# A heads' loop in a written order for TensorE, with dt's columns in the values' product

## The chip, the cores and the metric

The kernel runs on one core of one Trainium2 chip. The metric is the device time of one execution in microseconds, the median of three runs.

## What is computed

The reference is a chain of transformer blocks on 512 tokens of width 1024 in fp32: first a block with a pooling mixer, sparse attention, attention to a memory and a gated feed-forward, and then two hybrid layers. Only the hybrid layers are touched here. Each of them computes, from the same input `h`:

```python
proj = einsum("bld,de->ble", x, w_in)
q, k, v, z_attn, z_ssm, xbc, dt_raw = split(proj, ...)   # 1024, 256, 256, 1024, 1024, 1536, 16 columns
attn = sliding_window_attention(q, k, v, sinks) * silu(z_attn)
xbc = silu(causal_depthwise_conv(xbc, conv_w, conv_b))   # width 4
xs, bm, cm = split(xbc, ...)                             # 1024, 256, 256 columns
dt = softplus(dt_raw + dt_bias); a = -exp(a_log)         # 16 heads
# in chunks of 128 tokens, 2 groups of 8 heads, head width 64, state 128:
a_cs = cumsum(dt * a)                                    # within a chunk
y_diag = (cb * exp_segsum(a_cs)) @ (xs * dt)             # cb = C B^T
states = B^T @ (exp(a_cs_last - a_cs) * xs * dt)         # carried from chunk to chunk: prev
y_off  = (C @ prev) * exp(a_cs)
ssm = gated_rmsnorm(y_diag + y_off + xs * d_skip, z_ssm, ssm_norm_w)
out = concat([attn, ssm]) @ w_out                        # then a layer norm of ALPHA * x + out
```

## The kernel before, in words

Activations lie with channels on the 128 partitions and the 512 tokens along the free dimension, as eight tiles. Every fp32 operand of a projection is split into a high and a low part, and a projection of 128 output channels, called a unit here, is 24 products of 128x128 by 128x512: eight times high by high and high by low (L149, L150 in `mm3`) and eight times low by high (L154). A unit's weights come by one transfer of 512 KB on SyncE's queue (L104 in `weights`), are cast to the high part by ScalarE (L107) and give the low part by two VectorE subtractions of 512 columns (L110). There are three buffers each for the raw weights, the high and the low parts. PSUM has eight banks: four named mm for units, two named lg and two named tr.

A planner orders the instructions of TensorE, VectorE, ScalarE and GpSimd at build time by its own estimate of durations, with program order as the priority. Only SyncE's queue keeps program order (`manual_schedule` in `build`). Each engine then runs its list in order.

`hybrid(L)` goes through these steps.

1. The weights of dt (16 columns) are loaded and split into `wdt` (L914 to L919).
2. Four gate units (z_ssm) are done in two halves of 256 tokens with their weights held (`units_by_k`); `silu` follows (tanh on ScalarE, L211, and one VectorE operation, L911).
3. dt: 16 products of 128x48 by 128x512 (L931) into a tile of 16 partitions by 512 tokens, with the channels' high and low parts side by side. Softplus, the product with a, and the cumulative sum (a VectorE scan, L949) run on 16x512 tiles. The cumulative sum and its exponential are written to DRAM (`acsd`, L951, L953). Eight small transposes (L959, L960) bring dt and the sum to tokens on partitions (`dtok`, `atok`); `cdec` and `dend` follow.
4. Convolutions: `conv(j)` is a unit, one ScalarE operation that reads it (L900), three VectorE operations (L902), tanh (L211), and a last VectorE operation (L905). B and C take four, xs eight. cb (L979) and the transposes of B (L990) stand between them.
5. `tokens(g)` for each group of eight heads: for four chunks, four transposes of xs (L1007) into a tr bank, from which VectorE makes `xdt` (L1010) and, for three chunks, `xe` (L1014); a state product (L1016) into an lg bank, and VectorE's two operations that carry the state on (L1021, L1022).
6. `decay_rows(j)` asks on SyncE's queue for the broadcast rows of two heads (L1030, L1031). `decay(j)` makes exp of the clipped difference: four operations of 128 columns per head, on ScalarE (L1057) or, for the first head of a pair from the fourth pair on, on VectorE (L1055), an exponential (L1058), and a product with cb on GpSimd for the first and VectorE for the second head of a pair (L1059).
7. `heads(j)` for a pair of heads: eight products (L1070, recorded as 16) and three (L1076, recorded as 6), each group into a tr bank, and three VectorE operations (L1078, L1079, L1080). The product with the gate (L1110) and the sum of squares (L196, L199, with GpSimd's addition L200) follow; `gated_norm` runs once for each four pairs.
8. The loop over eight pairs holds seven more units: three convolutions and four gates. After it come two units for the keys (split to four tiles each, with copies between partition halves asked for on ScalarE's queue, L1126), then the values: tokens on the output partitions, 96 products of 128x128 by 128x256 (L1139 to L1141), then the second gated norm and the first queries' unit.
9. The attention loop (`scores`, `transposed`, `values`), and the output projection.

Of the kernel before, what the change touches and what calls it, by code (L numbers as in the profile page):

```python
# [61 lines left out]
class Kern:  # L62
# [79 lines left out]
    def mm3(self, out, w, xs, m=P, start=True, stop=True, woff=0):  # L142
# [732 lines left out]
    def l2_consts(self):  # L875
# [4 lines left out]
        self.small = self.load("small16", [16, 4], nc.sync)  # L880

    def hybrid(self, L):
# [4 lines left out]
        e16 = lambda: self.f("G")[:16, :]  # L887
        xr, e, uu, sm, dtf, acs, seg = (e16() for _ in range(7))
        nc.scalar.dma_start(seg, a["segs"])

# [4 lines left out]
        def conv(j, tag, w=None):  # L895

            y, o = self.f("ht"), self.f(tag)
            cw = lambda w: cwh[:, w * 12 + j : w * 12 + j + 1]
            pt = self.proj(W[4 + j], h, w=w)
# [17 lines left out]
        nc.gpsimd.memset(wdt.bitcast(F32), 0.0)  # L917
        w3, wd3 = wdt.rearrange("p (k m) -> p k m", m=48), wd.rearrange("p (k m) -> p k m", m=16)
        self.split(wd3, w3[:, :, :16], w3[:, :, 32:])  # L919

# [11 lines left out]
        nc.scalar.activation(xr, pt[32:48], AF.Identity, bias=self.small[:, L : L + 1])  # L932
        nc.vector.tensor_tensor(xr, pt[:16], xr, ALU.add)
        BC = [conv(8 + j, "R") for j in range(4)]
# [9 lines left out]
        nc.vector.scalar_tensor_tensor(dtf, xr, 0.0, uu, ALU.max, ALU.add)  # L944
        av = self.s("av", (16, 1), 2)
        nc.scalar.activation(av, self.small[:, 2 + L : 3 + L], AF.Exp)
        nc.vector.tensor_scalar(av, av, -1.0, None, ALU.mult)
        nc.vector.tensor_scalar(e, dtf, av, None, ALU.mult)
        nc.vector.tensor_tensor_scan(acs, seg, e, 0.0, ALU.mult, ALU.add)  # L949
# [48 lines left out]
        xdt = {}  # L998
        prevs = {}

        def tokens(g):

            for c in range(4):
                cc = slice(c * P, (c + 1) * P)
# [424 lines left out]
```

## Time and profile before

| | us |
|---|---|
| median of three runs (lowest, highest) | 1649.32 (1648.4, 1650.72) |
| the profiled execution | 1650.6 |
| its span, first to last instruction | 1648.8 |
| its mean granted clock of TensorE | 0.994 |

The span is what the trace shows; 1.8 us lie around it. In the stretch from about 800 us on the granted clock is 1.00 in the windows shown. A row of TensorE's timeline gives an instruction's start and duration; products overlap, so what a product costs is the distance of two starts. A number in brackets behind a row is the idle time of that engine just before it, and what ended it.

### The profile page before, as it was taken

Reading aid. Unit: us, or ns where it says so; the run is one execution under the profiler, and the core shown is the slowest. Engines: PE = TensorE matmul, PEld = TensorE weight load, DVE = VectorE, ACT = ScalarE, POOL = GpSimd, SP = SyncE. Lnnn points to the kernel's source line nnn. Section 1 sums busy time; section 2 is a strip of 40 time slices with the busy share of each in tenths; the row PEclk is TensorE's granted clock in tenths of the full one; section 3 lists DMA queues with packets and bytes.
Section 4 is the critical chain, followed back from the end, with each engine's and each line's share of the span. In section 5 each row is a group of like instructions: output and inputs, shape, how many; then the busy total and the mean of one; then the engine's idle time right before and its main releaser. Section 6 shows DMA issues by size and latency. Waiting matters only on the chain. (4 is left out here: it accounts for less than half of the span.)

```text
span 1648.8 us, 24498 instructions
## 1 busy us (share of the span) xinstructions
PE 1601.2 (97%) x9014; PEld 1358.7 (82%) x9014; DVE 1140.7 (69%) x2490; ACT 805.5 (49%) x1571; POOL 212.4 (13%) x251
## 2 busy tenths in 40 slices
PE   8999999999999999999999999999999989999996
PEld 5778888889898888888998778887998867888786
DVE  6779967547886455533767998765497799777447
ACT  4543245336863333323556556665355555666424
POOL 2000213000100000000000121211230022111131
PEclk9999999999999999999999999999999999999998
DMA  6522332243233323234636223211452522322133
GB/s 222 198 97 76 120 103 64 77 158 116 81 116 111 102 92 100 89 104 119 196 124 191 80 77 103 78 65 51 141 171 81 178 87 78 102 78 65 64 103 116
DMA packets 66233, 180.28 MB, mean 109 GB/s; under 512 B 7953, under 2 KB 19169, under 8 KB 66113
## 3 DMA queue, kind: packets, MB, share of 16 engines
q1 hardware_dynamic: 56320, 166.75, 31.8%
q10 hardware_dynamic: 9792, 11.96, 2.4%
q8 instruction: 71, 1.16, 0.3%
q14 instruction: 50, 0.40, 0.1%
HBM read 170.14 MB, written 9.06 MB: 109 GB/s over the span
## 5 line engine op out<-in xcount | busy, mean ns | idle before, releaser
L149 PE MATMUL psmm<-G,whi 128*128 128x512 f32 (+2 forms) x1244 | 479.2, 388 | 2.2 <-ACT whi L107 2.2
L110 DVE TENSOR_TENSOR wlo<-wraw,whi 128x512 fp32r<-128x512 f32 x515 | 358.8, 718 | 174.8 <-ACT whi L107 123.8
L150 PE MATMUL psmm<-G,whi 128*128 128x512 f32 (+2 forms) x1244 | 473.6, 384 | 0.0
L107 ACT CAST whi<-wraw 128x1024 fp32r<-128x1024 f32 (+3 forms) x262 | 267.7, 1024 | 339.7 <-PE psmm L150 272.3
L154 PE MATMUL psmm<-G,wlo 128*128 128x512 f32 (+2 forms) x1244 | 299.5, 382 | 0.0
L149 PEld LDWEIGHTS psmm<-G,whi 128*128 128x128 f32 (+1 forms) x1244 | 233.3, 188 | 50.3 <-issue 3.5
L150 PEld LDWEIGHTS psmm<-G,whi 128*128 128x128 f32 (+1 forms) x1244 | 233.2, 188 | 45.3 <-issue 1.5
L154 PEld LDWEIGHTS psmm<-G,wlo 128*128 128x128 f32 (+1 forms) x1244 | 228.2, 187 | 45.0
L149 PE MATMUL psmm<-R,whi 128*128 128x256 f32 (+1 forms) x684 | 210.4, 329 | 0.0
L150 PE MATMUL psmm<-R,whi 128*128 128x256 f32 (+1 forms) x684 | 210.1, 328 | 0.0
L149 PEld LDWEIGHTS psmm<-R,whi 128*128 128x128 f32 x684 | 130.0, 190 | 11.8 <-issue 0.3
L150 PEld LDWEIGHTS psmm<-R,whi 128*128 128x128 f32 x684 | 130.0, 190 | 11.5
L154 PE MATMUL psmm<-R,wlo 128*128 128x256 f32 (+1 forms) x684 | 130.3, 329 | 0.0
L154 PEld LDWEIGHTS psmm<-R,wlo 128*128 128x128 f32 x684 | 106.2, 190 | 11.5
L200 POOL TENSOR_TENSOR acc<-acc,sq 128x512 f32<-128x512 f32 (+1 forms) x42 | 53.0, 1261 | 475.4 <-ACT sq L199 475.3
L1176 ACT ACTIVATE w<-w,st 128x256 f32<-128x256 f32 (+1 forms) x128 | 59.9, 470 | 29.3 <-DVE st L1174 29.3
L211 ACT ACTIVATE sq<-ht 128x512 f32<-128x512 f32 (+1 forms) x48 | 29.4, 613 | 60.8 <-DVE ht L902 30.0
L902 DVE SCALAR_TENSOR_TENSOR ht<-psmm,cwh,ht 128x511 f32<-128x511 f32 (+2 forms) x72 | 53.4, 742 | 5.8 <-ACT ht L900 4.6
L836 DVE TENSOR_TENSOR sq<-psmm,G 128x512 f32<-128x512 f32 (+1 forms) x24 | 15.5, 646 | 56.0 <-PE psmm L154 56.0
L1172 DVE CUSTOM_DVE_ANT_0 w<-pslg,w,sinks 128x256 f32<-128x256 f32 (+1 forms) x128 | 51.5, 444 | 1.1 <-PE pslg L1167 0.6
L199 ACT ACTIVATE sq<-G 128x256 f32<-128x256 f32 (+1 forms) x76 | 35.1, 463 | 34.3 <-DVE G L1264 25.9
L1181 POOL TENSOR_SCALAR w<-w,st 128x256 f32<-128x256 f32 x64 | 37.9, 604 | 86.8 <-DVE st L1179 79.0
(332 smaller groups left out, 2597.3 us busy)
## 6 DMA issues: line engine op xcount, KB each, us to landing
wraw<-w_in SPq DMA_DIRECT2D x112, 512.0 KB, 3.4
wraw<-w_out SPq DMA_DIRECT2D x56, 512.0 KB, 3.8
wraw<-w_down SPq DMA_DIRECT2D x24, 512.0 KB, 3.5
wraw<-w_gate SPq DMA_DIRECT2D x22, 512.0 KB, 3.4
wraw<-w_up SPq DMA_DIRECT2D x22, 512.0 KB, 3.4
R<-acs SPq DMA_DIRECT2D x32, 256.0 KB, 5.7
wraw<-w_down SPq DMA_DIRECT2D x12, 384.0 KB, 3.7
wraw<-w_proj_attn SPq DMA_DIRECT2D x8, 512.0 KB, 3.4
```

What stands on the lines that cost most here:

```text
L107: nc.scalar.copy(hi[:, :n], raw[:, :n])
L110: nc.vector.tensor_tensor(lo[:, c], raw[:, c], hi[:, c].bitcast(F32), ALU.subtract)
L149: nc.tensor.matmul(out, whi[:, c], xh, start=start and k == 0, stop=False)
L150: nc.tensor.matmul(out, whi[:, c], xl, start=False, stop=False)
L154: nc.tensor.matmul(out, wlo[:, c], xh, start=False, stop=stop and k == n - 1)
L199: self.last_sq = nc.scalar.activation(t, src, AF.Square)
L200: (eng or nc.gpsimd).tensor_tensor(acc, acc, t, ALU.add)
L211: self.last_tanh = self.nc.scalar.activation(out, src, AF.Tanh, scale=scale)
L902: nc.vector.scalar_tensor_tensor(y[:, s:], pt[:, : S - s], cw(3 - s), y[:, s:], ALU.mult, ALU.add)
L1172: nc.vector.tensor_tensor_reduce(pr, pt, al[:, 256 - n :], 1.0, sink, ALU.add, ALU.max, mx[:, b : b + 1])
L1176: nc.scalar.activation(prs[b], prs[b], AF.Exp, bias=nm[:, b : b + 1], accum_out=sm[:, b : b + 1])
L1181: (nc.gpsimd if b % 2 else nc.vector).tensor_scalar(prs[b], prs[b], rc[:, b : b + 1], 1.0, ALU.mult, ALU.mult)
```

## The change

It has these parts.

- The weights of the values and dt lie together as `w_vdt`, 272 columns for each of eight channel tiles. The values' product stands directly after the gates, in three loads (three, three and two channel tiles), into four mm banks; its last 16 columns are dt, already with tokens on partitions. `dtb` and `alog` hold the biases and a_log broadcast to all partitions. dt's chain runs on tiles of 128x64; the cumulative sum is one product with the triangular matrix, and one transpose makes the rows that go to DRAM. The dt weights' split, its 16 products, the scan and the eight small transposes are gone. The rows in DRAM are now 64 rows of 128 elements, so a head's row of 512 tokens is read in four pieces.
- `unit` gives a unit's 24 products one by one, and `stream` runs eleven units so: the convolutions 4 to 7, four gates, the two keys, the first queries. A unit's weights are asked for when the unit before it begins.
- Tokens, states, heads' steps, gated norms and the counts of the units' products between them (`feed(n)`) are written out, and TensorE keeps this order (`manual_schedule` with PE), up to the end of the first queries' unit. `decay_rows(j + 3)` is asked for after the heads of pair j.
- All the clipped differences of `decay` are on ScalarE. `xe` has the buffers named rs in place of ht, and the values those named R in place of G.

The core of the diff:

```diff
+    def unit(self, w, xs):
+        whi, wlo = w
+        pt = self.ps()
+        def products():
+            n = len(xs)
+            for p in range(3 * n):
+                k = p // 2 if p < 2 * n else p - 2 * n
+                c = slice(k * P, (k + 1) * P)
+                lhs, rhs = (whi, xs[k][p % 2]) if p < 2 * n else (wlo, xs[k][0])
+                self.nc.tensor.matmul(pt, lhs[:, c], rhs, start=p == 0, stop=p == 3 * n - 1)
+                yield
+        return pt, products()
...
-        wd = self.s("w256", (P, 256), 9)[:, :P]
-        nc.sync.dma_start(wd, a["w_dt"][L])
-        wdt = self.s("wdt", (P, 48 * KD), 1, F32R)
...
-        pt = self.ps("lg")[:48]
-        for k in range(KD):
-            for n, x in enumerate(h[k]):
-                nc.tensor.matmul(pt, wdt[:, 48 * k : 48 * k + 48], x, start=k + n == 0, stop=k == 7 and n == 1)
-        BC = [conv(8 + j, "R") for j in range(4)]
+        vs = [self.f("R") for _ in range(2)]
+        pv = [self.ps() for _ in range(4)]
+        for c in range(3):
+            n = min(3, KD - 3 * c)
+            wh, wl = self.weights(a["w_vdt"][L][:, 816 * c : 816 * c + 272 * n], 272 * n)
+            for t, pt in enumerate(pv):
+                o, tt = pt[:, :272], slice(t * P, (t + 1) * P)
+                for kk in range(n):
+                    k = 3 * c + kk
+                    ws = slice(272 * kk, 272 * kk + 272)
+                    nc.tensor.matmul(o, h[k][0][:, tt], wh[:, ws], start=k == 0, stop=False)
+                    nc.tensor.matmul(o, h[k][0][:, tt], wl[:, ws], start=False, stop=False)
+                    nc.tensor.matmul(o, h[k][1][:, tt], wh[:, ws], start=False, stop=k == 7)
...
-        nc.vector.tensor_tensor_scan(acs, seg, e, 0.0, ALU.mult, ALU.add)
...
+        pa = self.ps("tr")
+        nc.tensor.matmul(pa[:, :64], self.tril, e, start=True, stop=True)
+        nc.vector.tensor_copy(atok, pa[:, :64])
+        prow = self.ps("tr")
+        nc.tensor.transpose(prow[:64, :P], atok, self.ident)
...
+        BC = [conv(8 + j, "R") for j in range(4)]
...
-            for e_, df in enumerate(dfs):
-                row = self.acsd[:, 2 * j + e_, :]
-                nc.sync.dma_start(df, row[:1].broadcast_to([P, S]))
...
+            rows_of = lambda i, hd, c, n: self.acsd[i, hd::16, :][c:].unsqueeze(0).broadcast_to([n, 4 - c, P])
             for e_, df in enumerate(dfs):
                 hd = 2 * j + e_
+                nc.sync.dma_start(df.rearrange("p (c l) -> p c l", l=P), rows_of(0, hd, 0, P))
...
-                    if cut:
-                        nc.vector.tensor_scalar(df[:, cc], df[:, cc], at, 0.0, ALU.subtract, ALU.min)
-                    else:
-                        nc.scalar.activation(df[:, cc], df[:, cc], AF.Relu, bias=at, scale=-1.0)
-                nc.scalar.activation(df, df, AF.Exp, scale=1.0 if cut else -1.0)
+                    nc.scalar.activation(df[:, cc], df[:, cc], AF.Relu, bias=at, scale=-1.0)
+                nc.scalar.activation(df, df, AF.Exp, scale=-1.0)
...
+        fill = [8, 9, 10, 11, 28, 29, 30, 31, 0, 1, 16]
...
+        def stream():
+            for u, e in enumerate(evict):
+                pt, products = self.unit(ahead.pop(0), h)
+                if fill and not ahead:
+                    ahead.append(self.weights(W[fill.pop(0)]))
+                for i, _ in enumerate(products):
+                    if i == 3 * KD - 1:
+                        e(pt)
+                    yield
...
+        def step(j):
+            if j < 7:
+                ws.append(decay(j + 1))
+            heads(j, *ws.pop(0))
+            if j < 5:
+                rows.append(decay_rows(j + 3))
...
+        ahead += [self.weights(W[fill.pop(0)]) for _ in range(2)]
+        rows = [decay_rows(0), decay_rows(1)]
+        with self.tc.manual_schedule(engines={mybir.EngineType.PE}):
+            for g, lead in ((0, 27), (1, 20)):
+                feed(lead)
+                tokens(g, 0)
+                tokens(g, 1)
+                if g == 0:
+                    ws.append(decay(0))
+                    rows.append(decay_rows(2))
+                feed(8)
+                state(g, 0)
+                tokens(g, 2)
+                feed(6)
+                state(g, 1)
+                tokens(g, 3)
+                feed(8 - 2 * g)
+                state(g, 2)
+                if g == 0:
+                    for n, j in ((3, 0), (24, 1), (22, 2)):
+                        feed(n)
+                        step(j)
+                else:
+                    for n, j in ((0, 3), (10, 4), (22, 5), (22, 6)):
+                        feed(n)
+                        step(j)
+                    feed(12)
+                    gated_norm(0, accs[0])
+                    feed(10)
+                    step(7)
+                    feed(2 + 24 + 8)
+                    gated_norm(1, accs[1])
+                    feed(16)
```

## Rows read from the trace of the kernel before

**Rows 1.** The page's first part: busy time in us, its share of the span and the number of instructions of each engine.

```profile
PE 1601.2 (97%) x9014; PEld 1358.7 (82%) x9014; DVE 1140.7 (69%) x2490; ACT 805.5 (49%) x1571; POOL 212.4 (13%) x251
```

**Rows 2.** The windows view: busy time of each engine in stretches of layer 0 (from 905.53) and layer 1 (from 1309.90). Columns: stretch, its length, then busy us and number of instructions of TensorE's products, its weight loads, VectorE, ScalarE and GpSimd, the granted clock, the share of the DMA engines and GB/s.

```profile
905.53:947.42 41.89, 38.29 (x210) 29.89 (x209) 36.90 (x61) 23.32 (x48) 7.21 (x5) 1.00 0.30 89
947.42:993.56 46.14, 42.88 (x256) 32.68 (x255) 44.04 (x75) 23.86 (x40) 14.41 (x9) 1.00 0.24 75
993.56:1005.07 11.51, 11.51 (x97) 11.51 (x96) 7.17 (x12) 5.01 (x7) 0.00 (x0) 1.00 0.60 166
1005.07:1013.75 8.68, 8.68 (x38) 6.57 (x37) 6.70 (x11) 6.19 (x10) 0.00 (x0) 1.00 0.33 114
1309.90:1351.67 41.77, 38.52 (x210) 30.06 (x209) 36.94 (x62) 23.52 (x48) 7.22 (x5) 1.00 0.31 93
1351.67:1397.80 46.13, 42.88 (x255) 32.67 (x254) 44.01 (x72) 23.14 (x38) 13.21 (x9) 1.00 0.23 72
```

**Rows 3.** The waits of TensorE between 854 and 1014 us, all of them: who waited for whom, us in total, times, longest us.

```profile
PE pslg L1016 <- DVE ht L1014: 3.1, 2, 1.9
PE pstr L1007 <- DVE G L905: 1.6, 1, 1.6
PE pstr L1070 <- DVE G L1078: 1.2, 2, 0.9
PE psmm L149 <- ACT whi L107: 0.5, 1, 0.5
PE pstr L206 <- DVE G L1078: 0.5, 1, 0.5
```

**Rows 4.** TensorE's timeline: the dt products and the unit after them; the first product of two units in a row; the first of the small transposes and the product after the last; two products of the values. Columns: start us, us, engine, line, operation, tiles, shape, count.

```profile
854.65 3.87 PE L931 MATMUL pslg<-G,wdt 128*48 128x512 f32 x16
858.36 0.39 PE L149 MATMUL psmm<-G,whi 128*128 128x512 f32 x1
...
863.82 0.39 PE L149 MATMUL psmm<-G,whi 128*128 128x512 f32 x1
...
869.26 0.39 PE L149 MATMUL psmm<-G,whi 128*128 128x512 f32 x1
...
880.24 0.23 PE L959 MATMUL pstr<-ident,G 16*128 16x16 f32 x1
...
880.83 0.50 PE L149 MATMUL psmm<-G,whi 128*128 128x512 f32 x1
...
993.67 0.28 PE L1140 MATMUL psmm<-wlo,G 128*128 128x256 f32 x1
993.79 0.28 PE L1141 MATMUL psmm<-whi,G 128*128 128x256 f32 x1
```

**Rows 5.** The timelines of ScalarE and VectorE at the end of layer 0's gates: the cast of the next unit's weights, and VectorE's low halves with the gates' operations between them.

```profile
853.65 1.05 ACT L107 CAST whi<-wraw 128x1024 fp32r<-128x1024 f32 x1 [7.47 <-PE psmm L176]
...
854.73 0.69 DVE L110 TENSOR_TENSOR wlo<-wraw,whi 128x512 fp32r<-128x512 f32 x1 [8.10 <-PE psmm L176]
855.34 0.74 DVE L911 SCALAR_TENSOR_TENSOR R<-R,psmm 128x256 f32<-128x256 f32 x2
856.00 0.68 DVE L110 TENSOR_TENSOR wlo<-wraw,whi 128x512 fp32r<-128x512 f32 x1
```

**Rows 6.** The timelines of TensorE and VectorE at the first group's tokens in layer 0: two chunks' transposes and the product after them, and VectorE's first scaled tokens for a state.

```profile
910.94 1.03 PE L1007 MATMUL pstr<-ident,G 128*128 128x128 f32 x8
911.73 0.48 PE L149 MATMUL psmm<-G,whi 128*128 128x512 f32 x1
...
916.24 0.68 DVE L1014 TENSOR_TENSOR ht<-pstr,dend 128x512 f32<-128x512 f32 x1
```

**Rows 7.** The timelines of TensorE and VectorE around the last convolution of layer 0, whose unit ends at 940.13: a heads' step and the product after it; the last operations of the convolution before it and of the last one.

```profile
940.13 1.09 PE L1070 MATMUL pstr<-R,G 128*64 128x128 f32 x14
...
941.84 0.47 PE L149 MATMUL psmm<-G,whi 128*128 128x512 f32 x1
...
941.29 1.77 DVE L905 SCALAR_TENSOR_TENSOR G<-sq,ht 128x512 f32<-128x512 f32 x1
...
948.74 0.68 DVE L905 SCALAR_TENSOR_TENSOR G<-sq,ht 128x512 f32<-128x512 f32 x1
```

**Rows 8.** Two rows of the timelines of VectorE and GpSimd, and three groups of the lines view from 905.53 to 1013.75 (busy us, mean ns of one, idle before).

```profile
939.00 2.37 DVE L110 TENSOR_TENSOR wlo<-wraw,whi 128x512 fp32r<-128x512 f32 x2
...
939.16 1.66 POOL L1059 TENSOR_TENSOR R<-R,R 128x512 f32<-128x512 f32 x1 [1.68 <-ACT R L1058]
...
L1055 DVE TENSOR_SCALAR R<-R,dtt 128x128 f32<-128x128 f32 x20 | 8.3, 439 | 0.0
...
L200 POOL TENSOR_TENSOR acc<-acc,sq 128x512 f32<-128x512 f32 x6 | 11.1, 1842 | 31.6 <-ACT sq L199 31.6
L1059 POOL TENSOR_TENSOR R<-R,R 128x512 f32<-128x512 f32 x7 | 9.9, 1412 | 36.8 <-ACT R L1058 36.8
```

**Rows 9.** The decay rows: the first request on SyncE's queue, the first ScalarE operation that reads them, that operation's mean, and the time of all these transfers to landing.

```profile
885.16 0.38 SPq L1030 DMA_DIRECT2D R<-acs  x1
...
897.70 0.42 ACT L1057 ACTIVATE R<-R,dtt 128x128 f32<-128x128 f32 x1
...
L1057 ACT ACTIVATE R<-R,dtt 128x128 f32<-128x128 f32 x31 | 10.1, 389 | 0.0
...
DMA to landing us min/median/max: 1.6/5.4/8.0
```

More of the change, by code (lines that the diff above doesn't have):

```diff
@@ L1032, in decay_rows @@
             return dfs, ee
-        for j in range(2, 4):
-            xs.append(conv(j, "G"))
-        xs.append(conv(4, "G"))
-        fill = [9, 10, 11, 28, 29, 30, 31]
-        wn = self.weights(W[fill[0]])
-        rows = [decay_rows(0), decay_rows(1)]
-        tokens(0)
         def decay(j):
             dfs, ee = rows.pop(0)
-            if j < 6:
-                rows.append(decay_rows(j + 2))
             for e_, df in enumerate(dfs):
                 hd = 2 * j + e_
-                cut = e_ == 0 and j >= 3
@@ L1088, in gated_norm, with gate_evict, feed @@
                 cat[8 + i] = self.pair(t, "R")
+        fill = [8, 9, 10, 11, 28, 29, 30, 31, 0, 1, 16]
+        evict = [lambda pt, j=j: xs.append(conv(j, "G", pt)) for j in range(4, 8)]
+        def gate_evict(pt):
+            zs.append(self.f("R"))
+            silu(zs[-1], pt)
+        evict += 4 * [gate_evict] + 2 * [lambda pt: keys(pt)] + [lambda pt: qs0.append(queries(0, pt))]
+        ahead = []
+        def stream():
[7 more added lines that the diff above has]
+                    yield
+        fillers = stream()
+        def feed(n):
+            for _ in range(n):
+                next(fillers)
         cat = [None] * 16
         accs = []
-        ws = decay(0)
-        for j in range(8):
-            g = j // 4
-            w = wn
-            if j < 6:
-                wn = self.weights(W[fill[j + 1]])
-            if j < 3:
-                xs.append(conv(5 + j, "G", w))
-            elif j < 7:
-                zs.append(self.f("R"))
-                silu(zs[-1], self.proj(None, h, w=w))
-            nxt = decay(j + 1) if j < 7 else None
-            if j == 3:
-                tokens(1)
-            heads(j, *ws)
-            ws = nxt
+        ws = []
+        def step(j):
[4 more added lines that the diff above has]
+                rows.append(decay_rows(j + 3))
             y = xs[j]
             nc.vector.tensor_tensor(y, y, zs[j], ALU.mult)
-            if j == 6:
-                gated_norm(0, accs[0])
             if j % 4 == 0:
@@ L1119, in hybrid, with keys @@
         kt = []
-        for j in range(2):
-            pt = self.proj(W[j], h)
+        def keys(pt):
             ks = [[self.r("G") for _ in range(2)] for _ in range(2)]
@@ L1142, in hybrid, with queries @@
-        for v, pt in zip(vs, pv):
-            nc.scalar.copy(v, pt)
-        gated_norm(1, accs[1])
+        def queries(j, pt=None):
+            pt = self.proj(W[16 + j], h) if pt is None else pt
+            qs = [self.r("G") for _ in range(2)]
+            for t, r, o in zip(qs, (top, bot), (bot, top)):
+                self.split(pt[r], t[r], t[o])
+            return qs
+        xe, qs0 = {}, []
+        for j in range(2, 4):
+            xs.append(conv(j, "G"))
+        ahead += [self.weights(W[fill.pop(0)]) for _ in range(2)]
@@ L1212, in values @@
             return pos
-        def queries(j):
-            pt = self.proj(W[16 + j], h)
-            qs = [self.r("G") for _ in range(2)]
-            for t, r, o in zip(qs, (top, bot), (bot, top)):
-                self.split(pt[r], t[r], t[o])
-            return qs
-        q = queries(0)
+        q = qs0[0]
         gate, pts = {}, {}
@@ L1357, in _constants @@
     c["dist"] = np.where((dd >= 0) & (dd < P), dd, 1e30).astype(np.float32)
-    seg = np.ones((16, S), np.float32)
-    seg[:, ::P] = 0.0
-    c["segs"] = seg
     return c
```

122 lines of the change are left out of this document (52 added, 70 removed).

## The prediction

> **What bounds the kernel now.** The page's busy times come first: TensorE is busy 1601.2 of 1648.8 us, VectorE 69% of it [rows 1]. Time can only come off by giving TensorE less to do or by taking away what little it waits. The windows by stage come next [rows 2]: the reader is to see that the heads' loop of layer 0 (905.53 to 993.56) holds 3.60 + 3.26 = 6.86 us in which TensorE did nothing, and that VectorE is 88% and then 95% full there, against 69% over the span. Layer 1's windows repeat it: 3.25 + 3.25 = 6.50 us. The waits of TensorE name the causes [rows 3]: all but 0.5 us end on VectorE, on the scaled tokens (xe), on a convolution's output, or on a PSUM bank that VectorE hadn't read yet. So the stretch has two limits close together, TensorE and, just behind, VectorE. 13.4 us of idle in both layers is the most that a better order can give.
>
> **Part 1: dt's columns go into the values' product.** The old dt product runs from 854.65 to 858.36: 16 products, 3.71 us, and nothing else runs on TensorE meanwhile [rows 4]. It goes. So do the eight small transposes, 880.24 to 880.83, 0.59 us [rows 4]. The 96 values' products get 272 columns instead of 256. A 256-column product is started every 0.12 us [rows 4], and 24 512-column ones take 5.44 us, 0.227 each [rows 4]; the difference is 0.107 us for 256 columns, so 16 columns cost 0.0067 us and 96 products 0.64 us. The cumulative sum as a matmul and one transpose are new. They are not in the trace; the nearest rows are the old small transposes (0.07 each) and the tokens' transposes (eight in 0.79 us [rows 6]), so I take 0.24 us for both, between 0.15 and 0.5. The chain of small operations on dt gets narrower tiles and lies beside the convolutions' products, as it does now with no wait in TensorE's list [rows 3]; nothing is counted for it.
>
> What the dt product also did was cover. The weight buffers of the gates are free only at the gates' end, so the next unit's split starts at 853.65 on ScalarE; its low halves are written by VectorE from 854.73 and, behind two gate operations, from 856.00 to 856.68 [rows 5]. TensorE passed from gates to dt at 854.65 and needed those halves only at 858.36 [rows 4]. In the new order the product that follows the gates is the values' one, which needs exactly such a split. Its first block needs the first low half for its second product (at about 854.78, ready about 855.3: 0.5 us), and its next block the second half (ready about 856.45, some 0.8 us after TensorE could use it). I take 1.4 us. Low bound 0.5 (both halves ahead of the gate operations), high bound 2.8 (both behind all four). Net of part 1 for a layer: 3.71 + 0.59 - 0.64 - 0.24 - 1.4 = 2.0 us; for two, **4.0 us**, bounds 1.2 to 5.9.
>
> **Part 2: the heads' loop by hand.** The same products are done (eleven units of 24, the tokens' transposes, the states, eight heads' steps of 1.71 us, as 940.13 to 941.84 [rows 7]), but in a written order, with the two keys' units and the first queries' as filler. The values leave this place (11.51 us [rows 2]) without changing its sum. The twenty VectorE subtractions of the decays go to ScalarE: 8.3 us less for VectorE [rows 8], and about 20 x 0.39 = 7.8 us more for ScalarE [rows 9], which was half idle (23.32 of 41.89 and 23.86 of 46.14 [rows 2]). VectorE's own account for layer 0: 36.90 + 44.04 + 7.17 + 6.70 = 94.81 us busy [rows 2], minus 8.3, minus the four low halves of the values' weights at about 0.7, makes 83.7. TensorE's: 108.22 - 11.51 - 6.86 = 89.85. So VectorE needs 6 us less than TensorE, but it will be 93% full, and every place where TensorE arrives early still waits. Place by place, with a product at 0.227 us:
>
> First state of the first group: from the end of the fifth convolution unit, TensorE has 3 products, the tokens' transposes (0.79 [rows 6]) and 8 products, 3.3 us. VectorE finished that convolution and the first scaled tokens 5.98 us after the same point (910.94 to 916.24 + 0.68 [rows 6]); then it didn't matter, because 23 products stood between. A wait of 2.7 by that row, 0 if the planner now lets the tokens go ahead of the convolution; I take the middle, 1.4. Tokens of the second group: 2 products, a heads' step and 20 products, 6.7 us, after the last convolution's end; now that output came at 949.42, 9.29 us after 940.13 [rows 7]. Of these 9.29, 1.77 was the preceding convolution's last operation, held by GpSimd [rows 7]; that convolution's unit lies a heads' step further ahead now, and no subtractions stand between. I take 0.9, between 0 and 2.6. State behind them: 1.2 us before (the 3.1 us of that wait less 1.9 [rows 3]), 0.3 now, with the subtractions gone. Third state and the fourth step right behind it: 0.5. The fifth step after only 10 products: 1.0, by the 0.9 of the PSUM wait [rows 3]. First gated norm: 0.3. Sum 4.4 us for a layer in place of 6.7, so 2.3 less, **4.6 us** for both; bounds below.
>
> **Part 3: weights ahead of decay rows.** In SyncE's queue a unit's weights already stand ahead of the next rows, and the rows have a lead: asked for at 885.16, first used at 897.70 [rows 9]. Their new source is in pieces of 512 bytes, four times as many packets. The rows take 5.4 us to land now [rows 9]; even at twice that they fit the 12.5 us, and at more they wouldn't. I count nothing, with 0 to 3 us as bounds.
>
> **Sum.** 4.0 + 4.6 = 8.6 us off. The profiled execution took 1650.6 (span 1648.8 and 1.8 around it) and lies 1.3 above the median of the runs, 1649.3; so 1642.0 for such an execution, and **1640.7** for a median.
>
> **Rivals.** (A) The order closes nearly all waits: one microsecond left in a layer. For it: 1.2 us of the idle is heads' steps that met at a PSUM bank [rows 3], and 22 to 24 products stand now between most steps. Against: VectorE at 93%. 4.0 + 2 x 5.7 = 15.4 off, 1633.9. (B) VectorE paces the stretch and the waits only move. In the two windows VectorE was 88% and 95% full and TensorE idle 8.6% and 7.1% [rows 2]; at 93% of 97 us (108.22 - 11.51) some 7 us would stay, which is no change, and part 1 alone remains: 1645.3, or 1648.1 if the first split costs 2.8. It also covers the case that the change doesn't do what it says, since the weights are ahead already. What speaks for it is GpSimd: a low-half pair took 2.37 us at 939.00, against 0.69 and 0.68 for single ones, while a GpSimd operation of 1.66 us ran from 939.16 [rows 5, 8]; all thirteen GpSimd additions and products of the two windows [rows 8] stay, in a shorter stretch. The Trainium skill ("SBUF — State Buffer", section "SBUF: two separate sides") states that VectorE with two SBUF inputs and GpSimd take a shared port pair as an exclusive lock, held for a whole instruction; by that rule moving subtractions to ScalarE frees VectorE, but each GpSimd operation still holds it up in full, and the time would be B's 1645.3. Row 939.00 agrees with the rule.
>
> (C) Slower: a fixed order that runs ahead of VectorE. The place is the pair of token groups. All 6.7 us of the old waits would stay, with 2.7 (first state) and 2.6 (second tokens) new, the 1.9 of the third state [rows 3] a second time, and 0.9 at the fifth step beyond the old ones: 14.8 less about 2.4 that the spread of the steps surely ends (0.3, 0.9 and, with the bank, 1.2), 12.4 in a layer. With the first split at 2.8, part 1 gives 0.6: 12.4 - 6.7 - 0.6 = 5.1 more, 1659.5 for both layers. It decides from the point where the waits pass 6.7 + 2.0 = 8.7 us in a layer. Against it: VectorE has 11 us less to do in the stretch.
>
> **How the numbers follow.** 0.2%, 3.3 us, is about what a measurement of this kernel can tell from no change. Forecast, 1636 to 1645: 0.50. A, 1629 to 1636: 0.17. B, 1645 to 1650: 0.18, of which a sixth lies under 1646. C, above 1650: 0.15, most of it past 1652.6. Faster 0.50 + 0.17 + 0.03 = 0.70; same 0.15 + 0.02 = 0.17; slower 0.13. The range takes in A down to its ceiling and the lower part of C: 1629 to 1654.
>
> **What would show it.** Part 1: no dt product, the values' 96 products at 0.127 us right behind the gates, and a first wait there on the low half of about 1.4 us; a wait over 2.8 or none would refute the cover argument. Part 2: TensorE's idle time between the fifth convolution unit and the first scores at about 4.4 us in a layer, ended by VectorE at the first state and at the second tokens; if it's under 2, A holds, if about 7, B. VectorE's idle time there should be small either way, and its subtractions gone. Part 3: no wait of ScalarE on the rows' transfers; if ScalarE waits for them, the 512-byte pieces land late, and the forecast is wrong for a cause that I priced at nothing. Idle time that appears in the scores behind the stretch would also make it wrong.

## The result and the profile after

| | before | after |
|---|---|---|
| median of runs, us (lowest, highest) | 1649.34 (1648.4, 1650.72), 4 runs | 1664.76 (1663.79, 1669.18), 4 runs |
| the profiled execution | 1650.6 | 1664.07 |
| its span | 1648.8 | 1662.3 |
| its mean granted clock of TensorE | 0.994 | 0.987 |

The ratio is 1.0097, 95% interval 1.008 to 1.0114: slower. The forecast was 1640.7, with a range from 1629 to 1654.

The page of after: busy time of the engines (against [rows 1]), and the packets of the whole execution.

```profile
PE 1599.8 (96%) x8972; PEld 1358.2 (82%) x8972; DVE 1111.4 (67%) x2454; ACT 811.1 (49%) x1615; POOL 208.5 (13%) x249
...
DMA packets 82999, 180.23 MB, mean 108 GB/s; under 512 B 8176, under 2 KB 39872, under 8 KB 82880
```

TensorE and VectorE both have less to do than before, and still the span is longer. The same bytes moved in 82999 packets; before it was 66233, with 19169 under 2 KB.

The waits of TensorE in after, first in layer 0 (854 to 1030), then in layer 1 (1260 to 1440); they answer to [rows 3]. Columns: who waited for whom, us in total, times, longest us.

```profile
PE pslg L1038 <- DVE rs L1032: 8.1, 1, 8.1
PE pstr L1026 <- DVE G L919: 4.7, 1, 4.7
PE pstr L222 <- POOL acc L216: 2.3, 1, 2.3
PE psmm L947 <- DVE wlo L110: 0.2, 1, 0.2
...
PE pslg L1038 <- DVE rs L1032: 5.5, 1, 5.5
PE pstr L1026 <- DVE G L919: 4.8, 1, 4.8
PE pstr L222 <- POOL acc L216: 2.3, 1, 2.3
```

Three places hold nearly all of it: the first state of the first group (L1038), the first group's tokens (L1026, behind the fourth convolution's output), and the second gated norm (L222). Windows of after: the stretch from the first values' product to the first scores in both layers, and two pieces of it around the longest wait (columns as in [rows 2]).

```profile
853.67:1024.22 170.55, 155.18 (x829) 125.54 (x828) 121.03 (x204) 94.04 (x180) 21.06 (x15) 0.96 0.43 115
1266.14:1434.15 168.01, 155.19 (x829) 125.52 (x828) 121.04 (x203) 94.08 (x180) 21.10 (x15) 0.96 0.50 116
...
930.00:936.00 6.00, 0.00 (x0) 0.00 (x0) 5.46 (x9) 4.53 (x11) 1.27 (x1) 0.61 0.51 113
936.00:940.00 4.00, 3.46 (x8) 2.23 (x9) 2.17 (x4) 0.58 (x1) 0.00 (x0) 0.50 0.58 165
```

Length less busy time is TensorE's idle: 15.37 and 12.82 us, where before had 6.86 and 6.50. Before, the same stretch was 159.10 and 158.78 us with 466 unit products in it; after has 480, at 0.227 us each. Set to equal work it grew by 170.55 - 159.10 - 14 x 0.227 = 8.3 us and by 6.1, together 14.3 us. The profiled execution is 13.5 us longer, so all of the loss is here.

What the first two waits wait for is seen one engine further back. SyncE's queue in after, from 885 us: start, duration of the request, line (L1053 and L1054 ask for rows, L104 for weights).

```profile
899.96 4.22 SPq L1053 DMA_DIRECT2D R<-acs  x1
...
906.60 2.43 SPq L104 DMA_DIRECT2D wraw<-w_in  x1
...
915.09 0.90 SPq L104 DMA_DIRECT2D wraw<-w_in  x1
916.31 3.09 SPq L1053 DMA_DIRECT2D R<-acs  x1
919.50 4.74 SPq L1054 DMA_DIRECT2D R<-acs  x1
```

Over both layers, a row request of SyncE took 0.5 us in the median before, and 1.97 us at most; now the two kinds take 1.1 (L1053) and 2.0 us (L1054), and 4.8 at most. The 32 row requests and six weight requests of layer 0 take up 69 of the 74 us from 891.65 to 965.44 on that queue; before, the same 38 took 18 us (884.74 to 938.34). ScalarE's timeline shows who pays:

```profile
913.23 0.62 ACT L227 ACTIVATE sq<-ht 128x512 f32<-128x512 f32 x1
918.09 1.05 ACT L107 CAST whi<-wraw 128x1024 fp32r<-128x1024 f32 x1 [4.24 <-DMA wraw<-w_in]
...
919.35 0.76 ACT L914 ACTIVATE ht<-psmm,cwh 128x512 f32<-128x512 f32 x1
...
929.30 1.04 ACT L107 CAST whi<-wraw 128x1024 fp32r<-128x1024 f32 x1 [5.85 <-DMA wraw<-w_in]
...
930.55 0.76 ACT L914 ACTIVATE ht<-psmm,cwh 128x512 f32<-128x512 f32 x1
```

The casts wait for weights that haven't landed, 4.24 and 5.85 us; those asked for at 915.09 landed 14.1 us later and were cast at 929.30. ScalarE runs in order, so the convolutions' reads (L914) stand behind the casts, VectorE's part of the convolution behind those, and TensorE's tokens and state behind that. VectorE's timeline has the ends of it:

```profile
923.48 0.69 DVE L919 SCALAR_TENSOR_TENSOR G<-sq,ht 128x512 f32<-128x512 f32 x1
...
934.60 0.69 DVE L919 SCALAR_TENSOR_TENSOR G<-sq,ht 128x512 f32<-128x512 f32 x1
...
935.81 0.68 DVE L1032 TENSOR_TENSOR rs<-pstr,dend 128x512 f32<-128x512 f32 x1
```

The first is the fourth convolution's output, and TensorE's waiting transposes start at 924.23. The second is the fifth one's; the scaled tokens for the state (L1032) stand behind it, and the state starts at 936.54.

### The profile page after: what moved, and what is told of

Its sections match the earlier page's. It is cut to its first block, busy times and chain, and to the rows that moved or that the text cites. A ratio compares the mean times of both kernels' runs of the same rounds, so it can differ in the third digit from the quotient of the medians.

```text
span 1662.3 us, 24415 instructions
## 1 busy us (share of the span) xinstructions
PE 1599.8 (96%) x8972; PEld 1358.2 (82%) x8972; DVE 1111.4 (67%) x2454; ACT 811.1 (49%) x1615; POOL 208.5 (13%) x249
## 2 busy tenths in 40 slices
DMA packets 82999, 180.23 MB, mean 108 GB/s; under 512 B 8176, under 2 KB 39872, under 8 KB 82880
## 5 line engine op out<-in xcount | busy, mean ns | idle before, releaser
L110 DVE TENSOR_TENSOR wlo<-wraw,whi 128x512 fp32r<-128x512 f32 (+1 forms) x519 | 357.3, 709 | 206.8 <-ACT whi L107 176.5
L107 ACT CAST whi<-wraw 128x1024 fp32r<-128x1024 f32 (+4 forms) x264 | 268.4, 1018 | 379.4 <-PE psmm L150 276.4
L149 PE MATMUL psmm<-G,whi 128*128 128x512 f32 (+2 forms) x1068 | 408.5, 386 | 1.2 <-ACT whi L107 1.2
L150 PE MATMUL psmm<-G,whi 128*128 128x512 f32 (+2 forms) x1068 | 405.2, 383 | 0.0
L154 PE MATMUL psmm<-G,wlo 128*128 128x512 f32 (+2 forms) x1068 | 256.7, 381 | 0.0
L149 PEld LDWEIGHTS psmm<-G,whi 128*128 128x128 f32 (+1 forms) x1068 | 200.2, 188 | 41.5 <-issue 3.0
L150 PEld LDWEIGHTS psmm<-G,whi 128*128 128x128 f32 (+1 forms) x1068 | 200.4, 188 | 38.2 <-issue 0.7
L154 PEld LDWEIGHTS psmm<-G,wlo 128*128 128x128 f32 (+1 forms) x1068 | 195.3, 187 | 37.9
L154 PEld LDWEIGHTS psmm<-R,wlo 128*128 128x128 f32 x684 | 106.2, 190 | 11.5
L167 PE MATMUL psmm<-G,whi 128*128 128x512 f32 x352 | 97.1, 419 | 0.0
L167 PEld LDWEIGHTS psmm<-G,whi 128*128 128x128 f32 x352 | 68.2, 199 | 16.4 <-issue 2.9
L215 ACT ACTIVATE sq<-G 128x256 f32<-128x256 f32 (+1 forms) x76 | 35.1, 463 | 45.6 <-DVE G L1310 26.7
L1067 POOL TENSOR_TENSOR R<-R,R 128x512 f32<-128x512 f32 x16 | 21.2, 1323 | 265.4 <-DVE wlo L110 171.6
## 6 DMA issues: line engine op xcount, KB each, us to landing
R<-acs SPq DMA_DIRECT2D x32, 256.0 KB, 12.6
```

Of the source, the lines that this page charges most:

```text
L107: nc.scalar.copy(hi[:, :n], raw[:, :n])
L110: nc.vector.tensor_tensor(lo[:, c], raw[:, c], hi[:, c].bitcast(F32), ALU.subtract)
L149: nc.tensor.matmul(out, whi[:, c], xh, start=start and k == 0, stop=False)
L150: nc.tensor.matmul(out, whi[:, c], xl, start=False, stop=False)
L167: self.nc.tensor.matmul(pt, lhs[:, c], rhs, start=p == 0, stop=p == 3 * n - 1)
L215: self.last_sq = nc.scalar.activation(t, src, AF.Square)
```

## The experiments

The median of the runs of before was 1651.0 beside the first four kernels, 1650.73 beside the next four and 1651.08 beside the last. The line numbers are those of each kernel, a few on from after's or before's where lines were added.

**1. Rows whole again.** The change in all its parts, but a VectorE copy orders the columns by head ahead of the transpose, so that a head's row lies as one piece of 2 KB. A pair of heads then takes 2 x (128 + 64) = 384 packets, not 2 x (4 x 128 + 3 x 64) = 1408.

```diff
+        atr = self.s("atr", (P, 64))
+        nc.vector.tensor_copy(atr.rearrange("p (h c) -> p c h", c=4), atok.rearrange("p (c h) -> p c h", h=16))
-        nc.tensor.transpose(prow[:64, :P], atok, self.ident)
+        nc.tensor.transpose(prow[:64, :P], atr, self.ident)
...
-                nc.sync.dma_start(df.rearrange("p (c l) -> p c l", l=P), rows_of(0, hd, 0, P))
+                row = self.acsd[:, 4 * hd : 4 * hd + 4, :].rearrange("i c l -> i (c l)")
+                nc.sync.dma_start(df, row[:1].broadcast_to([P, S]))
...
```

> The changed kernel, with the rows in DRAM laid out by head again (one small VectorE copy turns the columns before the transpose), so that the decay rows are read as one piece of 2 KB for a partition instead of four of 512 bytes. Nothing else differs. Theory T (the four-piece rows hold SyncE's queue, the weights behind them come late, ScalarE's cast waits for them, and with it the convolutions' output): the waits before the first tokens (4.7 and 4.8 us) go, that of the first state falls from 8.1 and 5.5 to 1.4 to 2.7, the half clock behind them goes; 1636 to 1646 us. Rival H (the written order itself starts the tokens too early for VectorE): within 5 us of the changed kernel's 1664.8. Rival S (ScalarE is now too full): also within 5 us of 1664.8.

1644.54 us, ratio 0.9959 (0.9944 to 0.9974): 20 us below after, and faster than before. TensorE's waits between 854 and 1020 us, then the products behind the first of them, then the windows of the stretch in both layers:

```profile
PE pslg L1040 <- DVE rs L1034: 2.9, 1, 2.9
PE pstr L222 <- POOL acc L216: 2.4, 1, 2.4
```

```profile
922.89 1.13 PE L1040 MATMUL pslg<-rs,G 128*128 128x512 f32 x2 [2.85 <-DVE rs L1034]
...
925.69 1.02 PE L1040 MATMUL pslg<-rs,G 128*128 128x512 f32 x2
```

```profile
851.55:1008.21 156.66, 151.20 (x830) 122.70 (x829) 120.67 (x205) 93.81 (x180) 21.14 (x15) 1.00 0.41 125
1251.97:1411.66 159.69, 154.23 (x830) 124.46 (x828) 121.37 (x205) 94.05 (x180) 21.14 (x15) 0.98 0.40 123
```

The tokens' wait is gone, the state's went from 8.1 to 2.9, and the gated norm's stays, so that one isn't the rows'. ScalarE has no wait for a transfer left in the stretch. In layer 1 the same two waits were followed by a granted clock of 0.69 (1325 to 1330) and 0.68 (1400 to 1405), and its stretch has 3.0 us more of busy TensorE than layer 0's. The expectation that the half clock would go held in layer 0 alone.

**2. Before, with the rows cut.** The kernel before, with its rows written by chunk and read in four pieces of 512 bytes, and nothing else.

```diff
-                row = self.acsd[:, 2 * j + e_, :]
-                nc.sync.dma_start(df, row[:1].broadcast_to([P, S]))
+                hd = 2 * j + e_
+                nc.sync.dma_start(df.rearrange("p (c l) -> p c l", l=P), rows_of(0, hd, 0, P))
...
```

> The kernel before, with its decay rows written to DRAM by chunk and read in four pieces of 512 bytes; nothing else differs. Theory T: the same late weights, ScalarE waiting for transfers of weights in the heads' loop, 1655 to 1670 us. Rivals H and S: no change, 1646 to 1653 us.

1659.36 us, ratio 1.0057 (1.0039 to 1.0075): the pieces alone cost the old kernel 8.4 us. TensorE's waits between 1260 and 1430 us, where before had 1.56 us on the same output:

```profile
PE pstr L1009 <- DVE G L905: 8.5, 2, 6.3
```

The time is in the range of the first theory, but not by its mechanism. Here ScalarE waits for the rows themselves: 10.9 us from 1255 to 1430, against 2.3 for weights, and 3.2 us in layer 0, against none. Its timeline, and TensorE's longest wait:

```profile
1355.16 0.69 ACT L1060 ACTIVATE R<-R,dtt 128x128 f32<-128x128 f32 x2 [6.19 <-DMA R<-acs]
1355.76 0.76 ACT L900 ACTIVATE ht<-psmm,cwh 128x512 f32<-128x512 f32 x1
...
1361.94 1.33 PE L1009 MATMUL pstr<-ident,G 128*128 128x128 f32 x5 [6.30 <-DVE G L905]
```

The convolution's read (L900) stands behind a decay that waits for its row, VectorE's part behind that, and the tokens behind VectorE.

**3. Cut rows, TensorE's order left to the planner.** After without `manual_schedule` for TensorE.

```diff
-        with self.tc.manual_schedule(engines={mybir.EngineType.PE}):
+        with ExitStack():
```

> The changed kernel with TensorE's order left to the planner in place of the written order; the rows stay in four pieces. Theory T: the weights are as late as before, so the time stays high, 1655 to 1670 us. Rival H: the planner puts products where the written order waits, 1640 to 1650 us. Rival S: within 5 us of 1664.8.

1658.6 us, ratio 1.0041 (1.0021 to 1.0061), seven runs from 1651.39 to 1661.95: 6 us below after by the medians, and still slower than before. The longest wait of the tokens is 6.74 us in layer 0 and 4.99 in layer 1, and ScalarE's casts wait 10.9 us for weights in layer 0 (880 to 970): another order of TensorE doesn't undo what the transfers do.

**4. Whole rows and the planner's order.** The edits of 1 and 3 together.

> Both: rows in one piece and TensorE's order left to the planner. Theory T: 1638 to 1650 us; its distance to the run with whole rows in the written order is what the written order is worth. Rival H: as with four pieces in the planner's order, 1640 to 1650 us. Rival S: within 5 us of 1664.8.

1633.45 us, ratio 0.9896 (0.9881 to 0.9911), 11 us below experiment 1 and below the expected 1638 to 1650. The window of layer 0's stretch; layer 1's is alike, with 152.15 us and 1.03 idle:

```profile
857.22:1009.45 152.23, 151.19 (x829) 122.47 (x828) 122.97 (x203) 92.01 (x179) 20.49 (x15) 1.00 0.41 127
```

TensorE's idle in the stretch is 1.04 and 1.03 us, against 5.46 twice in experiment 1: 8.8 us, by the two waits that the written order holds. Another 3.1 us is the slower clock behind them in layer 1.

**5. Rows in two pieces of 1 KB.** 768 packets for a pair: a dose between. The rows of the exponentials are read whole here, 128 KB in place of 96.

```diff
-        nc.tensor.transpose(prow[:64, :P], atok, self.ident)
+        nc.vector.tensor_copy(atr.rearrange("p (k h c) -> p k h c", k=2, c=2), atok.rearrange("p (k c h) -> p k h c", k=2, h=16))
+        nc.tensor.transpose(prow[:64, :P], atr, self.ident)
...
+                nc.sync.dma_start(df.rearrange("p (c l) -> p c l", l=256), rows_of(0, hd, P))
...
```

> The changed kernel in its written order, with the rows in DRAM by pairs of chunks, so that a row is read in two pieces of 1 KB; the exponentials' tile is filled whole (two pieces in place of three of 512 bytes). A pair of heads takes 768 packets in place of 1408 (whole rows: 384). Theory T, by the number of packets: the four requests take SyncE's queue about 5 us in place of 10, less than a heads' step with its products (7 us), so the weights are in time: 1641 to 1650 us. Rival Q: any row read in pieces is slow, whatever their number: 1658 to 1666 us.

1645.63 us, ratio 0.9974 (0.9964 to 0.9984): about 1 us behind whole rows, where the 512-byte pieces are 20 behind. The DMA view from 888 to 968 us, of after:

```profile
q1 hardware_dynamic: 11822, 9.11, 48.3%
...
wraw<-w_in SPq DMA_DIRECT2D x8, 512.0 KB, 12.6
R<-acs SPq DMA_DIRECT2D x16, 256.0 KB, 13.4
```

The columns are the packets of SyncE's queue, MB and the share of the 16 engines' time that its packets took; then issues with the KB of one and the median us from request to landing. The same lines of the others:

| | packets | MB | share | rows landing, us | weights landing, us |
|---|---|---|---|---|---|
| before | 4631 | 9.76 | 42.5% | 5.7 | 4.5 |
| 1, whole rows | 4880 | 10.49 | 43.2% | 4.5 | 3.5 |
| 5, 1 KB pieces | 8110 | 11.55 | 54.7% | 7.2 | 6.9 |
| after, 512 B pieces | 11822 | 9.11 | 48.3% | 13.4 | 12.6 |
| 2, before with 512 B pieces | 12574 | 9.78 | 55.5% | 12.0 | 11.8 |

At 101 packets in a microsecond (8110 / 80) a transfer lands in 7 us, and TensorE waits hardly longer than with whole rows (3.1 us at the first state, 2.4 at the gated norm). At 148 and 157 it lands in 12 to 13, and the weights are hit as much as the rows. In after fewer bytes move in this stretch than before, so bytes are not what ran out. Rows in 512-byte pieces and a step of 7.4 us would ask for 1408 / 7.4 = 190 packets in a microsecond, more than any row of the table shows. Nor are the DMA engines full all the time. A window of after in layer 1 and one of before's rows:

```profile
1325.00:1335.00 10.00, 7.03 (x33) 5.61 (x31) 4.18 (x7) 5.03 (x12) 1.27 (x1) 0.96 0.91 151
900.00:904.00 4.00, 4.00 (x19) 3.30 (x19) 3.62 (x6) 4.00 (x12) 1.30 (x1) 1.00 1.05 305
```

Before, the engines are full (a share of 1.05) at 305 GB/s, and the rows land in 5.7 us; in after they are half busy over layer 0's stretch at 115 GB/s, with landings twice as long and more, and reach 0.91 in layer 1 at half the rate of before. Whether the number of packets or their size is what counts can't be told apart here, since both change together.

**6. Part 1 alone.** Before with dt's columns in the values' product, whole rows and the old loop.

```diff
-        wdt = self.s("wdt", (P, 48 * KD), 1, F32R)
...
+            wh, wl = self.weights(a["w_vdt"][L][:, 816 * c : 816 * c + 272 * n], 272 * n)
...
+                    nc.tensor.matmul(o, h[k][0][:, tt], wl[:, ws], start=False, stop=False)
...
```

> The kernel before with part 1 alone: the values and dt in one product of 272 columns after the gates, dt's chain on tiles of 128x64, rows whole; the heads' loop, the decays on VectorE, the order and the rows' requests are the old ones. By the prediction's own sum 2.0 us off in a layer, 4.0 in all (bounds 1.2 to 5.9). With the first split's wait at the 0.2 us that the changed kernel's trace has there, 3.2 in a layer, 6.4 in all. If it gains nothing, the gain of the whole-rows runs is the loop's alone.

1651.61 us, ratio 1.0005 (0.9996 to 1.0014): the same. The windows of the stretch and of an early one, in this kernel and then in before:

```profile
856.49:1014.48 157.99, 150.08 (x819) 120.89 (x817) 129.88 (x223) 87.34 (x158) 21.73 (x15) 1.00 0.40 124
1259.05:1416.07 157.02, 150.08 (x820) 120.90 (x818) 129.22 (x222) 87.36 (x158) 22.92 (x15) 1.00 0.41 125
400.00:480.00 80.00, 74.01 (x567) 70.74 (x566) 65.05 (x166) 55.47 (x152) 10.40 (x14) 0.96 0.25 83
```

```profile
854.65:1013.75 159.10, 152.24 (x836) 121.85 (x835) 135.80 (x223) 90.22 (x159) 23.34 (x16) 1.00 0.40 120
1259.22:1418.00 158.78, 152.28 (x836) 121.84 (x834) 136.42 (x222) 90.20 (x159) 21.73 (x15) 1.00 0.40 120
400.00:480.00 80.00, 74.96 (x585) 72.03 (x584) 67.07 (x172) 56.87 (x155) 10.49 (x14) 0.98 0.26 85
```

With 470 unit products against 466 in each, the stretch is shorter by 1.1 + 0.9 = 2.0 us in layer 0 and 2.7 in layer 1, 4.7 in all. The total doesn't show it, against the expected 4.0 to 6.4. In this profiled execution the stretch starts 1.8 us later (856.49 against 854.65), and that is not the change's doing: among the profiled kernels with the values' product first, the three with a granted clock of 0.96 from 400 to 480 us, ahead of any changed instruction, start at 856.5 to 857.2 (experiments 4, 5, 6), the two with 1.00 at 853.6 and 853.7 (experiment 7 and after). The tail behind the second stretch is 1.5 us longer, with four unit products fewer in it; behind both stretches TensorE waits 0.8 us for GpSimd (L1183), which it didn't before. The median of ten runs says that, start and tail included, nothing is left of the 4.7 us. Whether the change itself gives them back isn't settled by these runs.

**7. Other counts in the written order.** Experiment 1 with products moved: more between the first tokens and the first state, and ahead of the second gated norm.

```diff
-                feed(8)
+                feed(8 if g else 21)
...
-                    for n, j in ((3, 0), (24, 1), (22, 2)):
+                    for n, j in ((3, 0), (16, 1), (20, 2)):
...
-                    feed(2 + 24 + 8)
+                    feed(47)
                     gated_norm(1, accs[1])
-                    feed(16)
+                    feed(3)
```

> Whole rows in the written order, with the counts of products moved: 21 in place of 8 ahead of the first group's first state (then 5, 3, 16 and 20 in place of 8, 3, 24 and 22), and 47 in place of 34 ahead of the second gated norm (then 3). Theory: the two waits left there, 2.85 and 2.36 us in each layer, are places where TensorE comes early; both go, 10 us less than with the old counts, 1632 to 1637 us. Rival B (VectorE paces the whole stretch): the waits come back elsewhere, 1639 to 1646 us.

1635.18 us, ratio 0.9907 (0.9892 to 0.9922), 9.4 us below experiment 1. Both waits were too few products between two steps: TensorE's waits between 854 and 1020 us no longer name the gated norm, the idle of a stretch falls from 5.46 to 2.54 us in layer 0, the granted clock is 1.00 in both, and the first state is

```profile
PE pslg L1040 <- DVE rs L1034: 1.3, 1, 1.3
```

**8. VectorE gets its differences back.** Experiment 4, with the first heads' clipped differences from the fourth pair on given back to VectorE, as before.

```diff
-                    nc.scalar.activation(df[:, cc], df[:, cc], AF.Relu, bias=at, scale=-1.0)
+                    if e_ == 0 and j >= 3:
+                        nc.vector.tensor_scalar(df[:, cc], df[:, cc], at, 0.0, ALU.subtract, ALU.min)
+                    else:
+                        nc.scalar.activation(df[:, cc], df[:, cc], AF.Relu, bias=at, scale=-1.0)
```

> Whole rows in the planner's order, with the clipped differences of the first heads from the fourth pair on given back to VectorE, as in the kernel before. If VectorE is what TensorE waits for, 8 us more of it in a layer bring waits back: 2 to 8 us more than with all on ScalarE (1633.5). If it isn't, within 2 us of it.

1632.58 us, ratio 0.9887 (0.987 to 0.9903): the same as experiment 4 within the intervals. In this order, moving these operations to ScalarE was worth nothing. This and experiment 4 are the fastest versions measured.

**9. Weights asked for on another queue.** After, with its 512-byte pieces, but the weights of the stretch requested by ScalarE.

```diff
-                    ahead.append(self.weights(W[fill.pop(0)]))
+                    ahead.append(self.weights(W[fill.pop(0)], eng=nc.scalar))
...
```

> The kernel after, its decay rows still in 512-byte pieces on SyncE's queue; only the eleven weight requests of the stretch between the gates and the first scores go out on ScalarE's queue. Theory 1, the pieces fill one queue and what stands in it: the weights no longer stand behind rows, land in 3 to 5 us instead of 11.9, ScalarE's two waits of 10.1 us for them and the first tokens' 4.8 us of TensorE go away; the rows themselves still come late, so that part of the first state's wait stays; 1645 to 1655 us. Theory 2, the pieces fill something that both queues share: the weights land as late as before (10 us and more), ScalarE waits as long, and the time stays at 1658 to 1668 us.

1679.01 us, ratio 1.0165 (1.0148 to 1.0182): slower than either theory gave. The first requests, from 880 to 888 us (KB of one, median us to landing), and below them SyncE's longest wait from 880 to 980 us:

```profile
wraw<-w_in SPq DMA_DIRECT2D x1, 512.0 KB, 3.2
R<-acs SPq DMA_DIRECT2D x2, 256.0 KB, 12.3
wraw<-w_in ACTq DMA_DIRECT2D x1, 512.0 KB, 14.6
R<-acs SPq DMA_DIRECT2D x2, 96.0 KB, 16.6
```

```profile
SPq L1053 <- DMA wraw<-w_in: 35.1, 4, 17.3
```

The weights asked for at 879.97, just ahead of one pair's rows, land in 3.2 us; those asked for at 886.44, just behind that pair but in a queue of their own, need 14.6. The median of all weights from 880 to 1010 us is 11.5. So the pieces also slow transfers that stand in another queue: the second theory, as to landing. A full queue is not needed for it: SyncE's requests take up 30 us of the 110 from 880 to 990 here, and its rows still land in 10.9 us in the median. The total can't be read for it, because the split made new waits: row requests held until a weights' transfer landed (35.1 us in four waits; why a row request waits for one isn't shown), and ScalarE, which now waits 17.5 us for rows, issues its weight requests only behind those waits. TensorE's waits at the first tokens and the first state grew to 7.2 and 12.9 us. The Trainium skill ("DMA: Bandwidth & Descriptors", section "Issuing engines are not separate DMA queues") says that transfers started by different engines run on the same 16 DMA engines and interleave; the 14.6 us agree with that. The Trainium skill ("Perfetto Trace Analysis", section "DMA Optimizations") says that spreading requests over engines may help where making descriptors is the bottleneck, and that larger transfers do better than small ones. Here moving the weights' requests cost 11 us (by the ratios 1.0165 and 1.0097), though no run shows that descriptors were the bottleneck, and larger pieces gained 20.

## Why the prediction was wrong

**Part 3 failed, by the size of one term.** "I count nothing, with 0 to 3 us as bounds" stood for rows in pieces of 512 bytes; "even at twice that they fit the 12.5 us, and at more they wouldn't". Measured, that term is 20 us here (after against experiment 1 by the medians; 23 by their ratios to before), 25 in the planner's order (experiment 3 against 4) and 8.4 in the old loop (experiment 2). Little more than twice the landing came: 5.4 us [rows 9] became 12.0 in the median, 17.7 at most. Two things were missing. The lead of 12.5 us was that of the first rows, and the later ones were asked for into a path already full of pieces: 1408 packets for each pair of heads, when a heads' step with its 24 products comes every 7.4 us. And in after the rows were not the transfers that were mostly waited for. From 888 to 968 us ScalarE waited 1.7 us for rows and 10.1 us for weights that shared the path, and it is in order, so the convolutions' reads stood behind the casts. I priced the transfer that the change touches, by its own landing time, and not its neighbours. In the old loop it was the rows themselves that came late (10.9 us of ScalarE's waits in layer 1, experiment 2), so there the lead failed and not the neighbours. The text's own sign ("if ScalarE waits for them") was thus right for the old loop; in after it pointed at the right part and mostly the wrong transfer.

**The clock added to it.** Behind the 8.1 us of idle TensorE was granted 0.50, 1.2 GHz, from 936 to 940 (the window above), and 1.00 from 904 to 916, ahead of the waits. The timeline of after from the first wait on:

```profile
924.23 1.09 PE L1026 MATMUL pstr<-ident,G 128*128 128x128 f32 x5 [4.69 <-DVE G L919]
924.97 3.46 PE L167 MATMUL psmm<-G,whi 128*128 128x512 f32 x8
936.54 2.08 PE L1038 MATMUL pslg<-rs,G 128*128 128x512 f32 x2 [8.11 <-DVE rs L1032]
...
941.72 1.02 PE L1038 MATMUL pslg<-rs,G 128*128 128x512 f32 x2
```

From 936.54 to 941.72 it ran the same twelve products as experiment 1 between 922.89 and 925.69: 5.18 us against 2.80, so 2.4 us lost beside the idle time itself. The eight products behind the first wait took 3.46 us where experiment 1's took 2.08, another 1.4. Over both layers, after has 17.3 us more idle TensorE in the stretch than experiment 1 (28.2 against 10.9) and 4.9 us more of busy time on the same products; together 22.2 of the 22.5 us between the two profiled spans.

**Part 1 was near in the stretch and missing in the total.** 4.7 us in the stretch of experiment 6, forecast 4.0 (1.2 to 5.9), and nothing by the medians. (The bounds move the first split alone; with those of the new matmul and transpose, 0.15 to 0.5, they would be 0.7 to 6.0.) The values' product starts every 0.126 us, forecast 0.127. The first split was oversized: 1.4 us taken, bounds 0.5 to 2.8, and 0.2 us of wait came, below the low bound. With 0.2 in its place the sum gives 6.4, so the nearness of 4.7 to 4.0 is in part luck: 1.7 us that the other terms promised didn't come. Of these, 0.8 and 0.2 us is TensorE's wait at the first scores in the two layers, which the sum didn't have.

**Part 2 was near in sum, with other places.** Without the rows' term (experiment 1) TensorE idles 5.46 us in the stretch of each layer; 0.2 is the first split, so some 5.2 stand against the forecast 4.4. The first state is 2.85 in place of 1.4: the row's own 2.7 was right, and the middle with zero was a hope that the planner would put tokens ahead of the convolution. The second gated norm, 2.36 behind GpSimd's addition, wasn't foreseen; the text looked at the first one (0.3). The second tokens, the state behind them, the third state and the fifth step, 2.7 us together, came to nothing that a wait row shows. The sum of the two parts, 8.6 us, came out somewhat smaller: experiment 1 is 6.5 us below before by the medians, and its median lies 3.8 us above the 1640.7. Its stretches, set to equal work as above, are 5.6 and 2.3 us shorter than before's, 7.9 in all, and layer 1's lost 3.0 us to the clock. The profiled execution, 9.0 us below before's, is the fastest of its four runs.

**Rivals.** C gave 1659.5 and the right sign for the wrong cause: of its new waits only the first state's 2.7 exists, and a fixed order that runs ahead of VectorE costs 9 to 11 us against a better one (experiments 4 and 7), yet not against before. A, 1633.9, is what the parts give with whole rows and a better order: 1633.45 and 1635.18. B is refuted, though experiment 1's 1644.54 lies within 1 us of its 1645.3, which is chance: VectorE doesn't pace the stretch, since moved counts alone cut the idle from 5.46 to 2.54 us with VectorE busy 123.4 us in place of 120.7 (experiment 7) and giving it the subtractions back cost nothing (experiment 8). The rule of the Trainium skill ("SBUF — State Buffer", section "SBUF: two separate sides") that stood with B may hold for single rows as 939.00 [rows 8], but the time that it was read to give, 1645.3, isn't what happened: in experiment 4 GpSimd ran 20.5 us in that stretch and TensorE idled 1.04.

**What stays open.** Which resource the pieces fill, with the DMA engines 43 to 58% busy in after's windows, but for 91% in ten microseconds of layer 1; whether packets or their size count; and where part 1's gain goes in experiment 6.

## What to carry to other kernels

When a change cuts a broadcast or strided transfer into smaller pieces, count packets per microsecond for the whole core beside the bytes, and look both at whether the transfer itself still lands in time for its later uses and at who waits for the other transfers in flight and what stands behind that waiter on an in-order engine. A small copy that makes the source contiguous (here one VectorE copy of 128x64) can be worth more than the change that cut it. And a written order of products is read best by its leftover waits: each named 2 to 3 us, of which moving a dozen products removed one and halved the other.

## What the runs showed of the hardware

With 512-byte pieces at about 150 packets in a microsecond, a 512 KB transfer landed in 12 us instead of 3.5, with the DMA engines 48% busy over 80 us of layer 0; 1 KB pieces at 101 in a microsecond moved more bytes (145 GB/s against 115) and landed in 7. A row request on SyncE's queue grew from 0.5 us in the median to 1.1 and 2.0 with it. A 512 KB transfer in another queue was slowed alike (14.6 us). Behind 8.1 us of idle, TensorE's granted clock was 0.50 for 4 us, and twelve products took 5.18 us against 2.80; after a wait of 2.85 us in experiment 1 the clock stayed at 1.00 in one layer and was 0.69 over 5 us in the other.
